# A hybrid encoder block on one core: the opening's transfers as contiguous blocks, and three pieces of the second feed-forward in another form

## The chip, the cores and the metric

The kernel runs on one core of a Trainium2 chip. Its time is the device time of one execution in microseconds. An execution that the hardware profiler recorded gives the rows quoted here; line numbers such as L157 are lines of the kernel before.

## The reference

One layer on a residual stream x of 256 tokens by 2048 features, all in float32:

```
x = x + 0.5 * swiglu(rms_norm(x, ffn1_norm), ffn1_w_up, ffn1_w_down)     # D_FF = 5632
h = rms_norm(x, mix_norm); proj = h @ w_in                               # two recurrent branches, gated
x = x + merged @ w_out
x = x + cross_attention(rms_norm(x, xattn_norm), rms_norm(mem, mem_norm), wq, wkv, wo)
x = x + 0.5 * swiglu(rms_norm(x, ffn2_norm), ffn2_w_up, ffn2_w_down)
return rms_norm(x, final_norm)

def swiglu(h, w_up, w_down):
    gate, up = split(h @ w_up, 2);  return (silu(gate) * up) @ w_down
```

The change lies in the start of the first feed-forward and in the weights of the second.

## The kernel before

**Precision.** A float32 operand is split into a high part (ACT, L156: a copy into the matmul's number type) and a low part (VectorE, L157: the original less the high part). A product takes three matmuls: high by high, low by high (both at L593, or L587 in the opening) and high by low (L595, or L590).

**The feed-forward.** The up-projection runs in 11 groups of 512 hidden columns. A group has 8 pieces; a piece is a block of weights of 128 partitions by 2048 columns (1 MB), in four quarters of 512 columns, and belongs to two of x's 16 feature tiles. The order of pieces, and of the down-projection's pieces put between the groups, is written out in `ffn_order`: in the second feed-forward a group runs its pieces as 1, 3, 4, 0, 2, 5, 6, 7; behind groups 1 and 2 stand two down pieces each, behind later groups four.

A "fast" piece does a two-by-two block product with seven products in place of eight. For this it needs differences of the weight quarters. Where they come from depends on the piece:

- made on the spot: the 1024 KB piece is loaded (L308) and VectorE computes the four differences, in three operations, at L314 (1024 columns), L316 and L317 (512 each), into a second tile;
- "ready": the differences were computed during the middle of the kernel (`make_ahead`, L210: a load on POOL's queue, four subtractions at L218, a store to DRAM at L219). The feed-forward then loads three quarters of the piece (768 KB, L304) and the prepared tile (1024 KB, L306), and VectorE only splits (1536 columns at L157, then twice 1024).

`sums_ready` (L88) says which pieces of the second feed-forward are ready: in groups 0 to 2 all fast ones, in odd later groups all but 0, 5, 7, in even ones all but 0, 3, 5, 7. That makes 58 tiles prepared ahead. In `beside` they are taken up in turns, every two to four weight pieces of the middle stage.

**Tiles and queues.** All weight loads go out on SP's queue, two pieces ahead of the product (`weights`). The loaded tiles come from two pools, three and (in the second feed-forward) two tiles, taken in a fixed turn; a piece of either form takes two. A load waits until the last reader of the tile's earlier content is done. The high parts have three tiles of 2048 columns, and a fast piece uses two of them. The engines run their own queues in order. The order in each queue is made by the compiler's scheduler, but SP, ACT and VectorE keep the written order for the first eight weight pieces (`manual_schedule`).

**The opening.** `xT` holds x by features: per partition 512 columns (x's first block: feature tiles 0 and 1, 256 tokens each), 16 columns of gains, then the other blocks. `head_x(0)` loads the first 528 columns in one transfer (L735), and ACT makes the high parts of both halves, z = 0 and 1, scaled by the gain (L738). `prepare` then takes the first weight piece in four quarters (L290): the high part of quarter 0 is made by VectorE (L292), which also makes the low part of x's two halves (L295) and of the quarter (L297); the other quarters go through `split`. The following three weight pieces are also loaded in quarters, each after another block of x (L742, 512 columns); for x's later use ACT scales the blocks at L534 and splits them at L156.

The first piece's products pair x's first half with quarters 0 and 1 and its second half with quarters 2 and 3 (`PRODUCTS["plain"]`).

Of the kernel before, what the change touches and what calls it, by code (L numbers as in the profile page):

```python
# [8 lines left out]
F32 = mybir.dt.float32  # L9
F32R = mybir.dt.float32r  # L10
ACT = mybir.ActivationFunctionType
ALU = mybir.AluOpType

P = 128
T = 256
D = 2048
KT = D // P
# [69 lines left out]

def sums_ready(name, e):  # L88

    made = () if e[1] < 3 else (0, 5, 7) if e[1] % 2 else (0, 3, 5, 7)  # L90
    return name == "ffn2" and e[0] == "fast" and e[2] not in made


# [1 line left out]
def block_kernel(ctx: ExitStack, tc: tile.TileContext, xT, xin, memT, vec, gfin, bgate, lruw, wu1, wd1, win, wv,  # L95
                 wg, wab, wout, wq, wk, wvm, wo, wu2, wd2, out_):
    nc = tc.nc
    pe, dve, act, sp = nc.tensor, nc.vector, nc.scalar, nc.sync
# [56 lines left out]
    def split(h, l, raw):  # L155
        done["high"] = act.activation(h, raw, ACT.Copy).ins  # L156
        done["low"] = dve.tensor_tensor(out=l, in0=raw, in1=h.bitcast(F32), op=ALU.subtract).ins  # L157
# [120 lines left out]
    def prepare(src, kind, cuts=1):  # L278

        if kind == "added":  # L280
            raw, l = begun.pop(0)
            h = hp.tile([P, 2048], F32R, name="h", tag="h")
            done["high"] = act.activation(h, raw, ACT.Copy).ins
            return h, l
        raw = raw_tile()
        n = 2048 // cuts
        if kind == "plain":
            h, l = split_tiles()
            for a in range(0, 2048, n):
                sp.dma_start(raw[:, a:a + n], src[:, a:a + n])  # L290
                if opening and not pairs1[0][1] and not a and cuts > 1 and len(pairs1) == 1:
                    dve.tensor_scalar(out=h[:, :n], in0=raw[:, :n], scalar1=1.0, scalar2=None, op0=ALU.mult)  # L292
                    for z in range(2):
                        v = [t[:, z * T:(z + 1) * T] for t in opening]
                        dve.scalar_tensor_tensor(out=v[2], in0=v[0], scalar=gain1(z), in1=v[1].bitcast(F32),  # L295
                                                 op0=ALU.mult, op1=ALU.subtract)
                    done["low"] = dve.tensor_tensor(out=l[:, :n], in0=raw[:, :n], in1=h[:, :n].bitcast(F32),  # L297
                                                    op=ALU.subtract).ins
                else:
                    split(h[:, a:a + n], l[:, a:a + n], raw[:, a:a + n])  # L300
            return h, l
        if kind == "ready":
            src, t = src
            sp.dma_start(raw[:, 512:], src[:, 512:])  # L304
            td = raw_tile()
            sp.dma_start(td, t)  # L306
        else:
            sp.dma_start(raw, src)  # L308
            if "raw2" in scoped:
                td = raw_tile()  # L310
            else:
                td = scoped["wide"].tile([P, 2048], F32, name="td", tag="wide")
            two = [v[:, a:a + 1024].rearrange("p (i n) -> p i n", i=2) for v, a in ((td, 0), (raw, 512))]
            dve.tensor_tensor(out=two[0], in0=raw[:, None, :512].broadcast_to([P, 2, 512]), in1=two[1],  # L314
                              op=ALU.subtract)
            dve.tensor_tensor(out=td[:, 1024:1536], in0=raw[:, 1024:1536], in1=td[:, :512], op=ALU.subtract)  # L316
            dve.tensor_tensor(out=td[:, 1536:], in0=raw[:, 1536:], in1=td[:, 1024:1536], op=ALU.subtract)  # L317
        h, l = split_tiles()
        if kind != "fast added":
            split(h[:, 512:], l[:, 512:], raw[:, 512:])  # L320
        else:
            act.activation(l[:, 512:], raw[:, 512:], ACT.Copy, scale=-1.0)
            nc.gpsimd.dma_start(l[:, 512:], src[:, 512:], accum_op=ALU.add)
            done["high"] = act.activation(h[:, 512:], raw[:, 512:], ACT.Copy).ins
        th = hp.tile([P, 2048], F32R, name="h", tag="h")
        if "wide" in scoped:
            tl = scoped["wide"].tile([P, 2048], F32R, name="tl", tag="wide")
        else:
            tl = lp.tile([P, 2048], F32R, name="tl", tag="l")
# [389 lines left out]
    pairs1, sq1 = [], TokenSquares()  # L719

    xq, sums1, opening = {}, [], []

    def gain1(k):
        return opening[0][:, 512 + k:513 + k]

    def head_x(p):

        q = p // 2
        if p % 2 == 0:
            xq[q] = slot(name="xf"), slot(name="xg"), []  # L730
        src, xg, out = xq[q]
        a = p % 2 * 512
        if p == 0:
            opening.append(slot(name="xf")[:, :528])
            sp.dma_start(opening[0], xT[:, :528])  # L735
            opening.extend((slot(F32R, "xh"), slot(F32R, "xl")))
            for z in range(2):
                act.activation(opening[1][:, z * T:][:, :T], opening[0][:, z * T:][:, :T], ACT.Copy, scale=gain1(z))  # L738
            sums = None
            pairs1.append(((opening[1], opening[2]), None))  # L740
            return
        sp.dma_start(src[:, a:a + 512], xT[:, 16 + p * 512:16 + (p + 1) * 512])  # L742
        if p == 1:
            operand_pairs([opening[0][:, :512]], gain1, 0, xg, out, made=opening[1:])
            pairs1[0] = out[-1]
        if p == 6:
            sp.dma_start(vt[:, :small_n], vec[:, :small_n])
        sums = operand_pairs([src[:, a:a + 512]], gain1, q, xg, out)
        if p % 2:
            sums1.append(sums)  # L750
        pairs1.append(out[-1])
# [111 lines left out]
    v = [scoped["extra"].tile([P, 1024], F32, name=f"v{t}", tag="extra") for t in range(2)]  # L863
# [468 lines left out]
def _layout(inputs):  # L1332
    import numpy as np

    a = {k: np.asarray(v) for k, v in inputs.items()}
# [26 lines left out]
    def first(gain, t):  # L1362

        t = features(t)
        return np.concatenate([t[:, :512], vector(gain), t[:, 512:]], axis=1)

    def vector(t):
        return t.reshape(-1, P).T
# [7 lines left out]
    for name in ("ffn1_norm", "mix_norm", "xattn_norm", "mem_norm", "ffn2_norm", "hgrn_norm", "conv_w", "conv_b"):  # L1376
# [7 lines left out]
    s, t = np.arange(P)[:, None] % 32, np.arange(32)[None, :]  # L1384
# [13 lines left out]
        "gfin": np.ascontiguousarray(np.broadcast_to(a["final_norm"], (P, D))),  # L1398
        "bgate": bgate,
        "lruw": np.ascontiguousarray(lruw).reshape(P, 16 * P),  # L1400
        "wu1": up(a["ffn1_w_up"][0]), "wd1": down(a["ffn1_w_down"][0]),
        "win": win, "wv": rows(w[:, 2048:3072]), "wg": wg, "wab": wab, "wout": rows(a["w_out"][0]),
        "wq": columns(a["xattn_wq"][0]), "wk": columns(wkv[:, :D]), "wvm": rows(wkv[:, D:]),
        "wo": rows(a["xattn_wo"][0]),
# [23 lines left out]
```

## Time and profile before

| what | value |
|---|---|
| median of 3 runs | 2415.89 us (2414.18 to 2417.0) |
| the profiled execution | 2416.49 us |
| its span, first to last instruction | 2414.7 us |
| instructions | 30834 |
| mean granted TensorE clock | 0.999 |
| moved by DMA | 684.34 MB, mean 283 GB/s |

The page lists for each engine its busy time and the number of instructions; PEld is TensorE's loading of weights, which overlaps its matmuls; DVE is VectorE. In rows of the timeline the first number is the start from the beginning of the span, the second how long it took, both in us; in brackets at the end stands the idle time of the engine just before, and what ended it. A row can hold several instructions (x4). In the rows by line stand busy us and mean ns of one, then the idle time before them and its releasers.

### The profile page before, as it was taken

How to read it: one execution, taken by the hardware profiler on the slowest of the kernel's cores; microseconds unless marked ns; L12 is line 12 of the kernel's file. 1: busy time of each engine (PE TensorE's matmuls, PEld its weight loads, DVE VectorE, ACT ScalarE, POOL GpSimd, SP SyncE). 2: the span in 40 equal slices, each digit the busy share in tenths (PEclk: the TensorE clock that was granted, in tenths of full speed). 3: DMA queues.
4: the chain of work that ended last, by engine and by line, in shares of the span. 5: the costliest groups of instructions: out<-in, count | busy, mean ns of one | idle time of the engine just before them, and what ended most of it. 6: DMA issues, size and time to landing. Idle time of an engine off the chain costs nothing.

```text
span 2414.7 us, 30834 instructions
## 1 busy us (share of the span) xinstructions
PE 2400.2 (99%) x12102; PEld 2003.2 (83%) x12102; DVE 2051.1 (85%) x2293; ACT 1466.9 (61%) x1502; POOL 102.3 (4%) x166
## 2 busy tenths in 40 slices
PE   9999999999999999999999999999999999999998
PEld 8888888888888888888888888888888788788887
DVE  7999999999866878688876777777789899999995
ACT  8567777777654454476434555455676666666664
POOL 0000000000000000000000000000000000000000
PEclk9999999999999999999999999999999999999999
DMA  8578999899858776878998899876797878787873
GB/s 314 195 230 257 276 277 277 275 274 271 270 215 320 275 284 245 302 283 317 349 332 332 305 356 343 320 291 242 262 348 303 285 283 288 257 293 277 290 276 146
DMA packets 102386, 684.34 MB, mean 283 GB/s; under 512 B 11360, under 2 KB 11616, under 8 KB 29280
## 3 DMA queue, kind: packets, MB, share of 16 engines
q1 hardware_dynamic: 78912, 519.82, 57.5%
q0 software_dynamic: 23328, 162.54, 22.2%
q8 instruction: 95, 1.56, 0.2%
q14 instruction: 51, 0.42, 0.0%
HBM read 619.40 MB, written 62.91 MB: 283 GB/s over the span
## 4 chain that ended last, share of the span: by engine, by line
PE 98%; DMA 1%; ACT 1%; DVE 0%; issue 0%; SPq 0%; ACTq 0%; DVEq 0%
PE acc L593 36%; PE acc L595 18%; PE acc L342 11%; PE acc L367 8%; PE acc L368 8%; PE acc L370 8%; PE acc L345 6%; PE acc L633 1%; PE acc L510 1%; DMA raw<-wu 1%; ACT h L156 0%; PE acc L949 0%; PE acc L1248 0%; PE acc L1202 0%; DMA raw<-t 0%; PE acc L1064 0%
## 5 line engine op out<-in xcount | busy, mean ns | idle before, releaser
L156 ACT ACTIVATE h<-raw 128x2048 fp32r<-128x2048 f32 (+3 forms) x577 | 866.8, 1528 | 622.4 <-PE acc L368 215.2
L157 DVE TENSOR_TENSOR l<-raw,h 128x2048 fp32r<-128x2048 f32 (+2 forms) x405 | 833.2, 2059 | 208.8 <-ACT h L156 208.1
L593 PE MATMUL acc<-h,xh 128*128 128x512 f32 x1220 | 475.0, 391 | 2.1 <-ACT h L156 2.1
L593 PE MATMUL acc<-h,xl 128*128 128x512 f32 x1220 | 473.0, 390 | 0.0
L593 PE MATMUL acc<-h,hidop 128*128 128x512 f32 x1408 | 352.1, 391 | 2.3 <-ACT h L156 2.3
L367 PE MATMUL acc<-h,ops 128*128 128x512 f32 x832 | 326.4, 392 | 0.0
L368 PE MATMUL acc<-h,ops 128*128 128x512 f32 x832 | 324.4, 390 | 0.0
L593 PEld LDWEIGHTS acc<-h,hidop 128*128 128x128 f32 x1408 | 262.4, 188 | 56.8 <-ACT h L156 3.2
L342 PE MATMUL acc<-ops,h 128*128 128x512 f32 x1152 | 277.5, 392 | 0.0
L593 PEld LDWEIGHTS acc<-h,xh 128*128 128x128 f32 x1220 | 229.0, 188 | 54.8 <-ACT h L156 7.0
L593 PEld LDWEIGHTS acc<-h,xl 128*128 128x128 f32 x1220 | 229.1, 188 | 46.6
L342 PEld LDWEIGHTS acc<-ops,h 128*128 128x128 f32 x1152 | 211.4, 188 | 41.3
L157 DVE TENSOR_TENSOR tl<-raw,h 128x1024 fp32r<-128x1024 f32 x172 | 203.6, 1218 | 14.5 <-ACT h L156 14.2
L370 PE MATMUL acc<-l,ops 128*128 128x512 f32 x832 | 205.6, 389 | 0.0
L156 ACT ACTIVATE h<-td 128x1024 fp32r<-128x1024 f32 x140 | 146.7, 1055 | 82.2 <-DVE td L314 31.1
L595 PE MATMUL acc<-l,hidop 128*128 128x512 f32 x704 | 190.4, 389 | 0.0
L370 PEld LDWEIGHTS acc<-l,ops 128*128 128x128 f32 x832 | 156.2, 188 | 32.4
L367 PEld LDWEIGHTS acc<-h,ops 128*128 128x128 f32 x832 | 156.2, 188 | 32.2
L368 PEld LDWEIGHTS acc<-h,ops 128*128 128x128 f32 x832 | 156.3, 188 | 31.4
L595 PE MATMUL acc<-tl,xh 128*128 128x512 f32 x624 | 178.1, 391 | 0.1
L157 DVE TENSOR_TENSOR tl<-td,h 128x1024 fp32r<-128x1024 f32 x140 | 170.0, 1219 | 8.4 <-ACT h L156 7.5
L595 PE MATMUL acc<-l,xh 128*128 128x512 f32 x600 | 165.6, 390 | 0.0
(262 smaller groups left out, 2493.0 us busy)
## 6 DMA issues: line engine op xcount, KB each, us to landing
raw<-wu SPq DMA_DIRECT2D x114, 1024.0 KB, 6.4
raw<-wd SPq DMA_DIRECT2D x88, 1024.0 KB, 6.4
prep<-wu POOLq DMA_DIRECT2D x58, 1024.0 KB, 6.6
t<-prep POOLq DMA_DIRECT2D x58, 1024.0 KB, 5.7
raw<-t SPq DMA_DIRECT2D x58, 1024.0 KB, 6.9
raw<-wu SPq DMA_DIRECT2D x58, 768.0 KB, 5.2
raw<-win SPq DMA_DIRECT2D x40, 1024.0 KB, 5.0
raw<-wg SPq DMA_DIRECT2D x32, 1024.0 KB, 5.0
```

The source lines that it names most:

```text
L156: done["high"] = act.activation(h, raw, ACT.Copy).ins
L157: done["low"] = dve.tensor_tensor(out=l, in0=raw, in1=h.bitcast(F32), op=ALU.subtract).ins
L342: pe.matmul(acc, h[:, k * P:(k + 1) * P], xs[k], start=k == 0, stop=False)
L345: done["product"] = pe.matmul(acc[:, :T], l[:, k * P:(k + 1) * P], xs[k][:, :T], start=False, stop=k == KT - 1).ins
L367: pe.matmul(accs[t], x[:, t * P:][:, :P], h[j], start=first and j == 0, stop=False)
L368: pe.matmul(accs[t], x[:, T + t * P:][:, :P], h[j], start=False, stop=False)
L370: done["product"] = pe.matmul(accs[t], x[:, t * P:][:, :P], l[j], start=False, stop=last and j == 3).ins
L510: pe.transpose(acc[:, z * T + t * P:][:, :P], tile[:, t * 512 + (2 * y + z) * P:][:, :P], ident)
L593: pe.matmul(acc, a, b, start=start, stop=False)
L595: pe.matmul(acc, ah, bl, start=False, stop=stop)
L633: pe.transpose(acc[:, z * T + t * P:][:, :P], hid[t][:, (2 * y + z) * P:][:, :P], ident)
```

## The change

**The layouts.** The host writes `xT` as one flat array of contiguous blocks: the 16 gain columns with x's first half (272 columns), x's second half (256), then seven blocks of 512. The first four pieces of the first up-projection's weights are written quarter by quarter, so that a quarter of 128 by 512 is one contiguous 256 KB block; before, its rows of 2 KB lay 8 KB apart.

**The opening's order.** SP issues x's first half, quarters 0 and 1, x's second half, then quarters 2 and 3. On ACT, the high part of x's second half is made behind quarter 1's; on VectorE its low part likewise.

**The second feed-forward.** In groups 1 and 2, piece 6 is made on the spot, not ready. In group 3, piece 0 is ready, not made on the spot. Groups 0 and 4 to 10 are as they were. 57 tiles are prepared ahead.

```diff
 def sums_ready(name, e):
-    made = () if e[1] < 3 else (0, 5, 7) if e[1] % 2 else (0, 3, 5, 7)
+    made = {0: (), 1: (6,), 2: (6,), 3: (5, 7)}.get(e[1], (0, 5, 7) if e[1] % 2 else (0, 3, 5, 7))
     return name == "ffn2" and e[0] == "fast" and e[2] not in made
...
             for a in range(0, 2048, n):
-                sp.dma_start(raw[:, a:a + n], src[:, a:a + n])
-                if opening and not pairs1[0][1] and not a and cuts > 1 and len(pairs1) == 1:
+                first = opening and len(pairs1) == 1 and cuts > 1
+                quarter = src.rearrange("p (a n) -> (p a) n", n=n)[a // n * P:][:P] if cuts > 1 else src
+                sp.dma_start(raw[:, a:a + n], quarter)
+                if first and not a:
                     dve.tensor_scalar(out=h[:, :n], in0=raw[:, :n], scalar1=1.0, scalar2=None, op0=ALU.mult)
-                    for z in range(2):
-                        v = [t[:, z * T:(z + 1) * T] for t in opening]
-                        dve.scalar_tensor_tensor(out=v[2], in0=v[0], scalar=gain1(z), in1=v[1].bitcast(F32),
-                                                 op0=ALU.mult, op1=ALU.subtract)
+                    remainder(0)
                     done["low"] = dve.tensor_tensor(out=l[:, :n], in0=raw[:, :n], in1=h[:, :n].bitcast(F32),
                                                     op=ALU.subtract).ins
                 else:
                     split(h[:, a:a + n], l[:, a:a + n], raw[:, a:a + n])
+                if first and a == n:
+                    sp.dma_start(opening[0][:, 272:], block(272, 256))
+                    rounded(1)
+                    remainder(1)
...
     def gain1(k):
-        return opening[0][:, 512 + k:513 + k]
+        return opening[0][:, k:k + 1]
+
+    def block(a, n):
+        return xT[a * P:(a + n) * P].rearrange("(p n) -> p n", p=P)
+
+    def rounded(z):
+        act.activation(opening[1][:, z * T:][:, :T], opening[0][:, 16 + z * T:][:, :T], ACT.Copy, scale=gain1(z))
+
+    def remainder(z):
+        dve.scalar_tensor_tensor(out=opening[2][:, z * T:][:, :T], in0=opening[0][:, 16 + z * T:][:, :T],
+                                 scalar=gain1(z), in1=opening[1][:, z * T:][:, :T].bitcast(F32), op0=ALU.mult,
+                                 op1=ALU.subtract)
...
-            sp.dma_start(opening[0], xT[:, :528])
+            sp.dma_start(opening[0][:, :272], block(0, 272))
             opening.extend((slot(F32R, "xh"), slot(F32R, "xl")))
-            for z in range(2):
-                act.activation(opening[1][:, z * T:][:, :T], opening[0][:, z * T:][:, :T], ACT.Copy, scale=gain1(z))
+            rounded(0)
...
-        sp.dma_start(src[:, a:a + 512], xT[:, 16 + p * 512:16 + (p + 1) * 512])
+        sp.dma_start(src[:, a:a + 512], block(16 + p * 512, 512))
...
+    def in_quarters(t):
+
+        t[0, :4] = t[0, :4].reshape(4, P, 4, 512).transpose(0, 2, 1, 3).reshape(4, P, 2048)
+        return t
...
-        "wu1": up(a["ffn1_w_up"][0]), "wd1": down(a["ffn1_w_down"][0]),
+        "wu1": in_quarters(up(a["ffn1_w_up"][0])), "wd1": down(a["ffn1_w_down"][0]),
```

More of the change, by code (lines that the diff above doesn't have):

```diff
@@ L741, in head_x @@
             return
-        sp.dma_start(src[:, a:a + 512], xT[:, 16 + p * 512:16 + (p + 1) * 512])
+        sp.dma_start(src[:, a:a + 512], block(16 + p * 512, 512))
         if p == 1:
-            operand_pairs([opening[0][:, :512]], gain1, 0, xg, out, made=opening[1:])
+            operand_pairs([opening[0][:, 16:]], gain1, 0, xg, out, made=opening[1:])
             pairs1[0] = out[-1]
@@ L1364, in first @@
         t = features(t)
-        return np.concatenate([t[:, :512], vector(gain), t[:, 512:]], axis=1)
+        blocks = [np.concatenate([vector(gain), t[:, :T]], axis=1), t[:, T:512]]
+        blocks += [t[:, i:i + 512] for i in range(512, KT * T, 512)]
+        return np.concatenate([b.reshape(-1) for b in blocks])
+    def in_quarters(t):
+        t[0, :4] = t[0, :4].reshape(4, P, 4, 512).transpose(0, 2, 1, 3).reshape(4, P, 2048)
+        return t
     def vector(t):
```

## The prediction

> **What bounds the kernel now.** I read the page first (busy times), then the chain of work that ended last, then the waits of TensorE (us in total, times, longest).
>
> ```profile
> PE 2400.2 (99%) x12102; PEld 2003.2 (83%) x12102; DVE 2051.1 (85%) x2293; ACT 1466.9 (61%) x1502; POOL 102.3 (4%) x166
> PE 98%; DMA 1%; ACT 1%; DVE 0%; issue 0%; SPq 0%; ACTq 0%; DVEq 0%
> PE acc L593 <- ACT h L156: 4.4, 4, 1.6
> PE acc L587 <- ACT h L156: 0.9, 1, 0.9
> ```
>
> TensorE is busy for 99% of the span and is 98% of the chain. The change takes no matmul away, so all that it can win is TensorE's pauses, and they are few: 0.9 us at L587, in the first piece, and 4.4 us in four waits at L593. The question is therefore where each pause comes from, and whether new ones come up. The timeline of TensorE gives their places.
>
> ```profile
> 5.44 0.70 PE L587 MATMUL acc<-h,xh 128*128 128x512 f32 x2 [0.22 <-DVE h L292]
> 7.51 0.73 PE L587 MATMUL acc<-h,xh 128*128 128x512 f32 x2 [0.93 <-ACT h L156]
> ...
> 1887.46 0.61 PE L595 MATMUL acc<-tl,xh 128*128 128x512 f32 x2
> 1889.69 0.50 PE L593 MATMUL acc<-h,xh 128*128 128x512 f32 x1 [1.61 <-ACT h L156]
> 1902.64 0.50 PE L593 MATMUL acc<-h,xh 128*128 128x512 f32 x1 [0.44 <-ACT h L156]
> 1911.55 1.43 PE L593 MATMUL acc<-h,hidop 128*128 128x512 f32 x5 [1.17 <-ACT h L156]
> ...
> 2095.55 0.96 PE L593 MATMUL acc<-h,hidop 128*128 128x512 f32 x3 [1.14 <-ACT h L156]
> ```
>
> The first two rows are the opening. The next four lie in group 3 of the second feed-forward (its pieces run from about 1867 us). The last is alone in a later group, which the change does not touch. A matmul's row is longer than its place in the row of matmuls: the chain has 20 of them in 4.53 us.
>
> ```profile
> 1863.98 4.53 PE acc L593 x20
> ```
>
> That is 0.227 us each, while single rows say 0.39, so each pause is really about 0.16 us longer than its idle column: after the two matmuls from 1887.46 the next was due at 1887.91 and came at 1889.69, which is 1.78. The three pauses of group 3 are 1.61 + 0.44 + 1.17 + 3 x 0.16 = 3.7 us; the opening's is 1.09, besides the late start at 5.44.
>
> **Opening: what is removed, added and moved.** Now one transfer brings 528 columns of x with the gains (264 KB), then four quarters of the first weight piece follow. The change sends 272 columns (136 KB), quarters 0 and 1, then x's other 256 columns (128 KB), then quarters 2 and 3. One issue by SP is added. L738 and L295 work in halves as now, but the second halves stand behind quarter 1's split. L295's second half (0.44 us) is hidden: the matmuls that need it come after twelve others.
>
> ```profile
> 0.74 0.38 SPq L735 DMA_DIRECT2D xf<-xT  x1
> 4.22 0.91 ACT L738 ACTIVATE xh<-xf 128x256 fp32r<-128x256 f32 x2 [1.78 <-DMA xf<-xT]
> 4.86 0.43 DVE L292 TENSOR_SCALAR h<-raw 128x512 fp32r<-128x512 f32 x1 [3.86 <-DMA raw<-wu]
> 6.83 2.01 ACT L156 ACTIVATE h<-raw 128x512 fp32r<-128x512 f32 x3 [1.71 <-DMA raw<-wu]
> 8.74 1.70 ACT L534 ACTIVATE xg<-xf 128x256 f32<-128x256 f32 x4
> 11.01 2.18 ACT L156 ACTIVATE h<-raw 128x512 fp32r<-128x512 f32 x4
> 11.96 0.19 PEld L593 LDWEIGHTS acc<-h,xh 128*128 128x128 f32 x1
> ```
>
> Three landings can be read here: x at 4.22, quarter 0 at 4.86, quarter 1 at 6.83. Quarter 0 came 0.64 us after x, quarter 1 took 1.97 for the same 256 KB. With 128 KB less in front, half of 0.64 is saved: quarter 0 lands at 4.54, and the first matmul starts 0.32 earlier, at 5.12. Quarter 1 then lands at 5.18 if it follows by 0.64, at 6.51 if it still takes 1.97. Its split on ACT takes 2.01 / 3 = 0.67, so TensorE goes on somewhere between 5.85 (no pause left: its four first matmuls last until 6.03) and 7.18. The first piece alone gains at least 0.32 and at most 0.32 + 1.09 = 1.41.
>
> What is late next is ACT: from 6.83 on its rows follow each other without idle to 11.01, the second piece's first split, and TensorE takes that piece up at 11.96. Half of L738 (0.46) now stands in this row of work. So the gain that goes on into the second piece is the advance of quarter 1 less 0.46: 6.83 - 5.18 - 0.46 = 1.2 at best, 0.32 - 0.46 = -0.14 at worst. SP's extra issue (0.38) is hidden by the transfers in flight; if it were not, quarters 2 and 3 would be that much later, still behind ACT. The rate over the first 16 us (40 slices of 0.4 us) says which end is nearer.
>
> ```profile
> GB/s 0 0 0 0 79 121 353 346 339 334 302 138 195 302 271 277 220 261 302 307 215 246 307 358 405 405 405 405 405 410 405 399 410 369 405 389 384 379 379 389
> ```
>
> Nothing moves before 1.6 us, then 340, then a trough of 138 to 307 from 4.4 to 8.8, then 405 with quarters of the same shape. The trough is where quarter 1 waits. Contiguous blocks may or may not fill it; less in front of quarter 1 helps either way. I take 1.1 us, near the upper end since 0.64 is the time that a quarter took outside the trough, and keep -0.1 to 1.4.
>
> The Trainium skill, DMA: Bandwidth & Descriptors, in Latency and other measured facts, has copies slowed by a large row pitch in HBM and advises contiguous tiles. Its slow pitches start at 512 KiB; here rows are 8 KB apart, and the 405 GB/s slices run at that pitch, so the rule does not reach this case; by it all 1.2 us would come. The skill's Perfetto Trace Analysis, DMA Optimizations, speaks against the split: DMAs under 2 KB carry an overhead each, and x's rows go from 2112 B to 1088 and 1024. If half a block took as long as the whole, the sum below would be smaller by 0.3.
>
> That the gain lasts needs cover too: VectorE is busy for 88.89 of the 89 us that follow.
>
> ```profile
> 39.00:128.00 89.00, 89.00 (x401) 73.35 (x400) 88.89 (x109) 56.73 (x54) 0.00 (x0) 1.00 0.55 203
> ```
>
> TensorE never pauses there, but a TensorE that is early could meet a VectorE that is not. VectorE's work starts with the same transfers, so I leave the 1.1 whole and count its loss in the range.
>
> **Second feed-forward.** A piece in the "ready" form loads 768 KB and 1024 KB of prepared differences; in the "fast" form it loads 1024 KB, and VectorE makes the differences at L314, L316, L317. Group 3's piece 0 goes from fast to ready; piece 6 of groups 1 and 2 goes from ready to fast. The price of one piece:
>
> ```profile
> 1882.51 1.22 DVE L314 TENSOR_TENSOR raw<-raw 128x1024 f32<-128x1024 f32 x1
> 1883.64 1.75 DVE L157 TENSOR_TENSOR l<-raw,h 128x1536 fp32r<-128x1536 f32 x1
> 1885.31 0.68 DVE L316 TENSOR_TENSOR raw<-raw,raw 128x512 f32<-128x512 f32 x1
> 1885.91 1.22 DVE L157 TENSOR_TENSOR tl<-raw,h 128x1024 fp32r<-128x1024 f32 x1
> 1887.05 0.69 DVE L317 TENSOR_TENSOR raw<-raw,raw 128x512 f32<-128x512 f32 x1
> 1889.67 1.76 DVE L157 TENSOR_TENSOR l<-raw,h 128x1536 fp32r<-128x1536 f32 x1 [1.94 <-ACT h L156]
> ```
>
> Three operations, 1.22 + 0.68 + 0.69 = 2.6 us of VectorE, against 768 KB of transfers. Which of the two is short, the busy times by stretch show (after TensorE and its loads: VectorE, ACT, POOL, clock, DMA share, GB/s):
>
> ```profile
> 1789.00:1809.00 20.00, 20.00 (x90) 16.57 (x89) 15.72 (x12) 13.01 (x12) 0.00 (x0) 1.00 1.01 411
> 1838.00:1858.00 20.00, 20.00 (x90) 16.57 (x89) 16.32 (x12) 13.08 (x13) 0.00 (x0) 1.00 1.01 423
> 1867.00:1887.00 20.00, 20.00 (x93) 16.55 (x92) 19.35 (x18) 10.39 (x10) 0.00 (x0) 1.00 0.70 247
> 1887.00:1912.00 25.00, 21.64 (x91) 16.39 (x90) 21.73 (x21) 16.45 (x15) 0.00 (x0) 1.00 0.75 282
> ```
>
> The ends of groups 1 and 2 (first two rows) have full queues and 4.3 and 3.7 us of free VectorE; group 3 (last two) has a full VectorE and queues at 0.7. The edit moves work from the full side to the free one in all three. In groups 1 and 2 I count the 2.6 us at nothing: the free VectorE time hides it; without that cover it would be 2.6 each.
>
> Group 3's pauses hang on the VectorE queue. The chain:
>
> ```profile
> 1877.51 1.76 DVE l L157
> 1879.70 8.35 DMA raw<-wu
> ...
> 1891.35 1.23 DVE tl L157
> 1892.59 6.94 DMA raw<-t
> 1899.64 2.96 ACT h L156 x3
> ```
>
> A VectorE split frees a tile, only then is the load issued, and it lands after TensorE wanted it; the next load hangs on the next split. Without piece 0's three operations VectorE is 2.6 us earlier from 1882.5 on. The ready form needs two loads for piece 0, whose second tile is free when the previous pieces are split, which by the order of the five tiles is about 1874 (an estimate), in queues at a 0.70 share; 768 KB at 247 GB/s cost 3.2 us of them, at 411 1.9. Piece 2's load then shares with less that is late, and VectorE's wait of 1.94 goes too or is halved. With 2.6 to 4.5 us of advance in VectorE's queue, the pauses at 1902 and 1911 (0.6 and 1.3) are covered; the first (1.78) has the load of piece 2 as its cause, which the same tile release starts. I take 3.5 of the 3.7; bounds 0 (only the place of the pause changes) and 3.7.
>
> Fifty-seven tiles are prepared ahead in place of 58, with the turns shifted by one; the stages where that is done have no pause in the waits above, so nothing.
>
> **Sum.** 1.1 + 3.5 + 0 = 4.6 us. The profiled execution took 2416.49 (span 2414.7, 1.8 around it), so 2411.9; the median shown is 0.6 lower, and from it I forecast **2411.3 us**, 0.19% less. A measurement of this kernel can tell about 0.2% from no change, 4.8 us: the forecast stands just at that line.
>
> **Rivals.** *More than the sum*: the pause at 2095.55 (1.14 + 0.16) goes as well, because what is early in group 3 stays early, and the opening gives its 1.4: 1.4 + 3.7 + 1.3 = 6.4, 2409.5. Against it: ACT's wait there is in a group with unchanged work.
>
> *Only one edit pays*: quarter 1 stays in its trough or VectorE eats the advance by 128 us, or piece 2's load stays late. Group 3 alone gives 2412.4, the opening alone 2414.8. For it: piece 2's two transfers hang on one tile release, which lies before 1882.5 and is not moved.
>
> *Slower*: an L314 stands at the head of VectorE's queue and waits for its 1024 KB, in groups 1 and 2, where the queues are at 1.01.
>
> ```profile
> L314 DVE TENSOR_TENSOR raw<-raw 128x1024 f32<-128x1024 f32 x28 | 34.1, 1219 | 7.2 <-DMA raw<-wu 7.2
> ```
>
> Now 28 such operations wait 7.2 us in all. Behind it stand the splits of piece 7 and of the down pieces, which free tiles, so SP's loads wait too. It decides once that wait and the 2.6 exceed the 4.3 or 3.7 us of free time. Then each group would pause as group 3 did: 2 x 3.7 - 1.1 = 6.3 more, 2422.2 (with group 3 no better). Against it: later groups run three or four fast pieces each with one pause in seven groups.
>
> *It does not do what it says*: the order in each queue is the scheduler's, and if it puts piece 0's loads late, group 3 is as before: the second rival's time.
>
> **Chances.** The forecast with its own range 2409.9 to 2412.9: 0.55, of it 0.32 past the 0.2% line (2411.06). More than the sum: 0.14. One edit or less: 0.13. Slower: 0.18, of it 0.01 within 0.2%. Faster by over 0.2%: 0.32 + 0.14 = 0.46; within: 0.23 + 0.13 + 0.01 = 0.37; slower: 0.17. The range 2408.0 to 2418.0 leaves out the slower case and some 0.02 below.
>
> **What would show it.** Quarter 1's split on ACT before 6 us and no idle at L587; VectorE without the L314 row in group 3's piece 0 and no TensorE idle from 1867 to 1912; in groups 1 and 2, L314 rows without idle ahead and VectorE near 18.5 of 20. I am wrong if TensorE shows a new wait for ACT or VectorE between 1789 and 1867, or near 128 us.

## The result and the profile after

| what | before | after |
|---|---|---|
| median | 2416.49 us (2414.18 to 2418.37) | 2411.79 us (2410.6 to 2414.4) |
| ratio of after to before | | 0.9982, 95% interval 0.9976 to 0.9988 |
| the profiled execution, its span | 2416.49, 2414.7 | 2412.53, 2410.8 |
| instructions, moved by DMA | 30834, 684.34 MB | 30823, 681.45 MB |

The kernel is 0.18% faster, some 4.3 us, and the forecast was 2411.3. The total came out; its terms did not all. In the kernel after, the lines that matter have moved: L587 is L590, L590 is L593, L593 is L596, L595 is L598, L290 is L292, L292 is L294, L304/L306/L308 are L307/L309/L311, L314/L316/L317 are L317/L319/L320, L680 is L683, L738 is L733, L534 is L537. Kernels made from the old one keep the old numbers.

From the page of after, the busy times:

```profile
PE 2399.4 (100%) x12102; PEld 2004.9 (83%) x12102; DVE 2048.3 (85%) x2292; ACT 1466.6 (61%) x1502; POOL 101.3 (4%) x164
```

TensorE is busy 0.8 us less than before in a span that is 3.9 us shorter: what went is mostly idle time. The waits of TensorE in after, and the places of its pauses in its timeline:

```profile
PE acc L596 <- ACT h L156: 2.6, 4, 1.2
```

```profile
4.92 0.92 PE L590 MATMUL acc<-h,xh 128*128 128x512 f32 x2
...
11.12 0.51 PE L596 MATMUL acc<-h,xh 128*128 128x512 f32 x1 [0.29 <-ACT h L156]
...
1801.66 0.50 PE L596 MATMUL acc<-h,xh 128*128 128x512 f32 x1 [0.90 <-ACT h L156]
...
1853.47 0.50 PE L596 MATMUL acc<-h,xh 128*128 128x512 f32 x1 [1.18 <-ACT h L156]
...
2091.90 0.96 PE L596 MATMUL acc<-h,hidop 128*128 128x512 f32 x3 [0.19 <-ACT h L156]
```

The wait at the first piece (0.9 us) is gone. Of the waits at the later pieces, the three of group 3 are gone; two new ones stand in groups 1 and 2, and the one at 2095 has shrunk from 1.14 to 0.19. Taking matmuls of equal number in both traces, after is ahead by 1.06 us at the second piece, by 0.70 to 0.77 from 48 to 1400 us, by 0.83 at 1752. Then it loses 1.2 in group 1 and 1.7 in group 2, gains 4.7 in group 3, 0.95 at 2095 and 0.33 later: 3.9 us in all, the difference of the spans.

The stretches of the three groups in after (1768.7 to 1818, to 1867, to 1912; in order: length, TensorE, its loads, VectorE, ACT, POOL, clock, DMA share, GB/s):

```profile
1768.70:1818.00 49.30, 48.40 (x218) 39.69 (x217) 45.81 (x43) 34.95 (x33) 0.00 (x0) 1.00 0.85 311
1818.00:1867.00 49.00, 47.82 (x214) 39.03 (x213) 45.83 (x42) 32.73 (x30) 0.00 (x0) 1.00 0.83 305
1867.00:1912.00 45.00, 45.00 (x204) 37.24 (x204) 43.40 (x41) 31.90 (x29) 0.00 (x0) 1.00 0.80 294
```

VectorE still has more than 3 us free in groups 1 and 2, though TensorE pauses there. VectorE's own rows show that it did not wait for data at the new operations; here the first of them in group 1 of after:

```profile
1793.99 1.22 DVE L317 TENSOR_TENSOR raw<-raw 128x1024 f32<-128x1024 f32 x1
...
1800.69 1.76 DVE L157 TENSOR_TENSOR l<-raw,h 128x1536 fp32r<-128x1536 f32 x1 [1.48 <-ACT h L156]
```

L317 (the old L314) has no idle time ahead of it. Over the whole span the made-on-the-spot form waits less than before, with one more of them:

```profile
L317 DVE TENSOR_TENSOR raw<-raw 128x1024 f32<-128x1024 f32 x29 | 35.4, 1219 | 5.4 <-DMA raw<-wu 5.4
```

What idles VectorE (1.48 us) is ACT, and ACT waits for a load. The chain of work through that place in after, and SP's queue:

```profile
1788.87 1.70 DVE l L157
...
1790.59 0.33 SPq L309
...
1790.96 8.11 DMA raw<-wu
...
1799.17 0.49 ACT h L156
```

```profile
1790.96 0.43 SPq L307 DMA_DIRECT2D raw<-wu  x1
```

This is piece 7, a ready piece behind piece 6, which is now fast. Its prepared tile (L309) is issued ahead of its own weights (L307), although the weights are wanted first. L309 waits for the tile that VectorE's split at 1788.87 frees; L307 stands behind it, shares the queues with 1024 KB of it, and takes 8.11 us. TensorE goes on at 1801.66. In group 2 the same pair goes out at 1841.90 and 1842.28, and L307's load takes 8.6 us. The profile puts ACT's wait there (until 1850.99) down to TensorE; by its 8.6 us the load landed at about the same moment. In the kernel before one place has this order: group 3's piece 2, the 8.35 us load of the prediction's chain, ahead of the pause at 1889.69. The new form of piece 6 brings that place into groups 1 and 2; the new form of piece 0 takes it out of group 3.

### The profile page after: what moved, and what is told of

Read it like the earlier page. It is cut to its first block, busy times and chain, and to the rows that moved or that the text cites. A ratio compares the mean times of both kernels' runs of the same rounds, so it can differ in the third digit from the quotient of the medians.

```text
span 2410.8 us, 30823 instructions
## 1 busy us (share of the span) xinstructions
PE 2399.4 (100%) x12102; PEld 2004.9 (83%) x12102; DVE 2048.3 (85%) x2292; ACT 1466.6 (61%) x1502; POOL 101.3 (4%) x164
## 2 busy tenths in 40 slices
DMA packets 102098, 681.45 MB, mean 283 GB/s; under 512 B 11328, under 2 KB 11840, under 8 KB 29248
## 3 DMA queue, kind: packets, MB, share of 16 engines
q8 instruction: 95, 1.56, 0.2%
## 4 chain that ended last, share of the span: by engine, by line
PE 97%; DVE 1%; DMA 1%; ACT 1%; issue 0%; SPq 0%; ACTq 0%
PE acc L596 36%; PE acc L598 18%; PE acc L345 11%; PE acc L370 8%; PE acc L371 8%; PE acc L373 8%; PE acc L348 6%; PE acc L636 1%; PE acc L513 1%; DMA raw<-wu 1%; DVE tl L157 0%; DVE l L157 0%; PE acc L962 0%; ACT h L156 0%; PE acc L1261 0%
## 5 line engine op out<-in xcount | busy, mean ns | idle before, releaser
L596 PE MATMUL acc<-h,xh 128*128 128x512 f32 x1220 | 476.0, 392 | 2.4 <-ACT h L156 2.4
L596 PE MATMUL acc<-h,xl 128*128 128x512 f32 x1220 | 473.6, 390 | 0.0
L596 PE MATMUL acc<-h,hidop 128*128 128x512 f32 x1408 | 352.3, 391 | 0.2 <-ACT h L156 0.2
L596 PEld LDWEIGHTS acc<-h,hidop 128*128 128x128 f32 x1408 | 262.8, 188 | 54.1 <-ACT h L156 0.6
L596 PEld LDWEIGHTS acc<-h,xh 128*128 128x128 f32 x1220 | 229.1, 188 | 55.5 <-ACT h L156 7.7
L596 PEld LDWEIGHTS acc<-h,xl 128*128 128x128 f32 x1220 | 229.3, 188 | 46.3 <-DVE xl L157 0.2
L598 PE MATMUL acc<-l,hidop 128*128 128x512 f32 x704 | 190.9, 390 | 0.0
L598 PE MATMUL acc<-tl,xh 128*128 128x512 f32 x624 | 177.6, 392 | 0.0
L598 PE MATMUL acc<-l,xh 128*128 128x512 f32 x600 | 165.7, 390 | 0.0
```

What stands on the lines that cost most here:

```text
L596: pe.matmul(acc, a, b, start=start, stop=False)
L598: pe.matmul(acc, ah, bl, start=False, stop=stop)
```

## The experiments

Two theories at the start. **T**: the order of the two loads of a ready piece makes a pause; the change moved the place. **V**: VectorE's row of work, with the tiles it frees, sets how much is lost; the order only says where. A third came after the first four runs. **D**: what group 3 needs is less to transfer in groups 1 and 2. Each kernel was timed beside the kernel before on the same chip. Intervals of 11 executions reach 0.09% (2.2 us) to either side, so the medians tell 3 us apart and not 1; the traces must do the rest, and each of them is one execution.

### The opening alone

```diff
-    made = {0: (), 1: (6,), 2: (6,), 3: (5, 7)}.get(e[1], (0, 5, 7) if e[1] % 2 else (0, 3, 5, 7))
+    made = () if e[1] < 3 else (0, 5, 7) if e[1] % 2 else (0, 3, 5, 7)
```

> The changed kernel with the old rule for the prepared pieces: the opening's edits alone. Theory A (the two edits add up): TensorE's second piece starts about 1 us earlier and 0.7 us of it is left at 48 us, as in the trace of the changed kernel; the pauses of group 3 (1.6 + 0.4 + 1.2 us idle) stand as before. Time 0.7 us under the kernel before, about 2415.8. Theory B (the opening's advance helps group 3 too): over 2 us under it.

2415.74 us against 2415.79: ratio 0.9998 (0.9990 to 1.0007). Nothing that the measurement can see. ACT's timeline in this kernel says why:

```profile
4.68 0.63 ACT L156 ACTIVATE h<-raw 128x512 fp32r<-128x512 f32 x1 [1.24 <-DMA raw<-wu]
...
8.11 1.28 ACT L156 ACTIVATE h<-raw 128x512 fp32r<-128x512 f32 x2 [2.00 <-DMA raw<-wu]
9.29 1.69 ACT L537 ACTIVATE xg<-xf 128x256 f32<-128x256 f32 x4
```

Quarter 1 is split at 4.68, earlier than my best bound. But ACT waits 2.00 us for quarter 2 and splits it only at 8.11, and its row of work, L537 onwards, begins at 9.29, later than the old kernel's 8.74. All transfers together are not slow here: they move 334 GB/s from 4.4 to 8.8 us, against 249 in before. Another transfer is the late one now, and no run tells why. TensorE starts the second piece at 12.22, against 12.18 in before.

### The second feed-forward alone

The new rule of `sums_ready` in the kernel before (the diff above, reversed).

> The kernel before with the new rule for the prepared pieces alone. Theory A (the edits add up): no pause in group 3, a pause of about 1 us in group 1 and one in group 2, about 3.2 us under the kernel before, 2413.3; the opening as before. Theory B: the pauses of groups 1 and 2 come of TensorE's advance from the opening; then they are missing here and it is 5 us under.

2413.16 us: 0.9989 (0.9980 to 0.9997), 2.6 us less. So the rule of the feed-forward gains by itself. In this trace the pauses stand where after has them, in groups 1 and 2, with none in group 3 (0.57 idle at 1802.18, 1.64 at 1854.28). The execution traced here took 2416.08, 2.9 us over this kernel's median; the places of the pauses are read from it, and not the gain.

It reached the second piece at 11.13, as early as after's 11.12, with the old opening; quarter 1 was split at 5.61, not 6.83. The same opening can be 1 us apart from one trace to another.

### The order of the two loads, in the kernel before

```diff
-            sp.dma_start(raw[:, 512:], src[:, 512:])
+            own = sp.dma_start(raw[:, 512:], src[:, 512:]).ins
             td = raw_tile()
-            sp.dma_start(td, t)
+            with tc.issue_after(own): sp.dma_start(td, t)
```

It swaps two rows of SP's queue, the pair of group 3's piece 2.

> The kernel before, with one thing changed: the load of a piece's own weights stands ahead of the load of its prepared tile on SP's queue, always. In the kernel before they stand the other way round at one place, piece 2 of group 3, behind piece 0. Theory T (order of issue): the pause of 1.78 us at that piece goes, since its 768 KB load no longer waits behind the other's tile; the later ones of group 3 shrink with it; 2 to 4 us under the kernel before. Theory V (VectorE's three operations): the pauses stay within 0.5 us in sum, the time is that of the kernel before.

2415.46 us: 0.9998 (0.9989 to 1.0007). The pause at 1889 is gone; the load that it waited for now takes 4.2 us, not 8.3. But the time has come back 16 to 20 us later in group 3. The chain behind the largest pause (1.49 idle):

```profile
1899.43 1.23 DVE tl L157
...
1900.67 7.01 DMA raw<-wd
...
1907.77 1.92 ACT h L156
...
1909.73 4.52 PE acc L593 x12
```

From 1880 to 1900 this chain runs through VectorE almost without a break; a VectorE split frees the tile for the down piece's load, which is late. The order of issue set the place of the pause, as T says, but not the loss, as V says. (Part of this execution's loss is a slower clock, told below.)

### The same order, in the kernel after

The same edit; it swaps the pairs of groups 1 and 2.

> The changed kernel, with the own weights' load always ahead of the prepared tile's. In the changed kernel they stand the other way round at two places, piece 7 of groups 1 and 2, behind piece 6. Theory T (order of issue): the pauses of 1.06 and 1.34 us there go, 2 to 2.4 us under the changed kernel, about 2409.5. Theory V (VectorE's 2.6 us in groups 1 and 2 are not hidden): the pauses stay, 2411.8.

2414.43 us: 0.9994 (0.9985 to 1.0003); no better than after. The pauses of groups 1 and 2 are gone (the two loads take 6.6 and 5.4 us), so the order was their immediate cause, but the 2.4 us did not come. The traced execution took 2412.65, 1.8 us under the median, and no less than after's. A new pause stands at the end of group 3 (1908.34, 1.56 idle), and its chain shows something new:

```profile
1905.89 0.60 ACT hid L683
1906.49 1.81 ACT h L156
...
1908.34 1.66 PE acc L596 x6
```

ACT's queue holds the copy of one of the group's finished sums out of its accumulator (L683) ahead of the split that TensorE needs next. L683 can only run when TensorE ends that sum; the split then takes 1.81 us, and TensorE stands still for most of it.

### The kernel after once more

No edit.

> The changed kernel once more, beside the variants below on one chip. Its pauses from 1768 to 1930 us should come out again as one of about 1 us each in groups 1 and 2 and none in group 3, and the time 3 to 5 us under the kernel before. If the opening's advance is steady, the second piece's first matmul stands at 11.1 us again; if it hangs on when the slow stretch of the transfers falls, anywhere from 11.1 to 12.2.

2412.63 us: 0.9986 (0.9977 to 0.9995). In this execution group 1 pauses for 1.86 us and group 2 not at all. Which of the two pauses is a matter of the execution; that they do is not. The order of the two loads is the same each time; what differs is how long the load behind takes. Here it is, in us from issue to landing, beside TensorE's pause behind it. The last four rows are runs told below; the run with two pieces in group 2 is left out, since its group 2 differs.

| trace | group 1: load, pause (idle) | group 2: load, pause (idle) |
|---|---|---|
| after | 8.1, 0.90 | 8.6, 1.18 |
| after once more | 9.1, 1.86 | 6.7, none |
| the feed-forward alone | 7.8, 0.57 | 9.1, 1.64 |
| only groups 1 and 2 | 8.0, 0.78 | 6.5, none |
| one piece in group 3 | 7.6, 0.39 | 7.8, 0.41 |
| order alone | 8.2, 0.98 | 6.4, none |
| contiguous blocks alone | 8.2, 0.98 | 6.3, none |

The pause grows with the load, and up to 6.7 us there is none. Why the same two transfers take longer one time than another, no run tells.

### Only group 3, and only groups 1 and 2

```diff
-    made = {0: (), 1: (6,), 2: (6,), 3: (5, 7)}.get(
+    made = {0: (), 1: (), 2: (), 3: (5, 7)}.get(
```

> The changed kernel, but piece 6 of groups 1 and 2 stays ready: of the rule's edits only that of group 3 is left, and 59 tiles are prepared. Theory V (VectorE's time sets it: 2.6 us less in group 3, nothing added elsewhere): no pause in groups 1 to 3, 2 to 2.4 us under the changed kernel. Theory D (the relief of the transfers in groups 1 and 2 is needed for group 3): pauses of 1 us or more stay in group 3, and the time is that of the changed kernel or worse.

2413.33 us: 0.9990 (0.9982 to 0.9999), 2.6 us less than before. Groups 1 and 2 do not pause; group 3 does, at 1899.65 (0.55) and 1909.46 (1.58). V's empty group 3 did not come, and D expected such pauses. The first hangs, as the one at 1902 in before, on a load that starts behind a VectorE split, though the three operations of piece 0 are gone from VectorE's queue:

```profile
1889.28 7.26 DMA raw<-t
...
1899.65 1.88 PE acc L596 x7
```

The second pause is again L683 ahead of the split. ACT's timeline here, and then in after:

```profile
1907.01 0.60 ACT L683 ACTIVATE hid<-acc 128x512 f32<-128x512 f32 x1 [2.71 <-PE acc L598]
1907.50 4.66 ACT L156 ACTIVATE h<-raw 128x2048 fp32r<-128x2048 f32 x3
```

```profile
1905.96 2.86 ACT L156 ACTIVATE h<-raw 128x2048 fp32r<-128x2048 f32 x2 [1.81 <-DMA raw<-wd]
1908.73 0.57 ACT L683 ACTIVATE hid<-acc 128x512 f32<-128x512 f32 x1
```

In after two splits stand ahead of L683. The order came out otherwise from another list of pieces, and the pause goes with the order.

```diff
-    made = {0: (), 1: (6,), 2: (6,), 3: (5, 7)}.get(
+    made = {0: (), 1: (6,), 2: (6,), 3: (0, 5, 7)}.get(
```

> The changed kernel, but group 3's piece 0 is made on the spot as before: of the rule's edits only those of groups 1 and 2. Theory V: the pauses of groups 1 and 2 (2.4 us) come on top of group 3's 3.7 or more, 2 us or more over the kernel before. Theory D: group 3's pauses shrink to 2 us or less, and it is no slower than before.

2414.89 us: 0.9996 (0.9988 to 1.0005). Group 1 pauses (0.78), and group 3 loses 1.7 (4.05 in before, 2.89 with the opening alone), the largest part at 1909.60 behind L683. V has the pauses of groups 1 and 2 come on top of group 3's, and they do not: this kernel has the edits of groups 1 and 2 without the relief of group 3, and is no slower than before. D fits better. The order of loads at group 3's piece 2 is before's here (1878.53 and 1878.91), and its load takes 7.4 us, but TensorE does not pause: the order makes a load late, and does not by itself make a pause.

### One piece fewer in group 3, one more in group 2

```diff
-    made = {0: (), 1: (6,), 2: (6,), 3: (5, 7)}.get(
+    made = {0: (), 1: (6,), 2: (6,), 3: (7,)}.get(
```

> The changed kernel with group 3's piece 5 ready too, so that only piece 7 is made on the spot there (58 tiles). Theory V: group 3 has no pause in the changed kernel, so nothing is won there; the pauses of groups 1 and 2 stay; the changed kernel's time within 1 us. If something of group 3 is still short, over 1 us under it.

2412.34 us: 0.9985 (0.9977 to 0.9994), equal to after within the intervals. Its pauses in groups 1 to 3 are small (0.39 and 0.41 idle, none in group 3; a split again stands ahead of L683), and its profiled span is the shortest, 2409.8.

```diff
-    made = {0: (), 1: (6,), 2: (6,), 3: (5, 7)}.get(
+    made = {0: (), 1: (6,), 2: (3, 6), 3: (5, 7)}.get(
```

> The changed kernel with a second piece of group 2 (piece 3) made on the spot, 2.6 us more for VectorE and 768 KB less to load. Theory V (VectorE has no free time left there): TensorE pauses 2 us or more longer in groups 2 and 3, about 2.6 us over the changed kernel. Theory D (the transfers are short): no longer pauses, the changed kernel's time or less.

2416.80 us: 1.0000 (0.9991 to 1.0009); the gain is used up. The pauses came late: 1911.63 (1.58, L683 ahead of the split at 1909.18) and in a later group, where the other traces pause for 0.39 us at most:

```profile
2034.49 0.96 PE L596 MATMUL acc<-h,hidop 128*128 128x512 f32 x3 [1.04 <-ACT h L156]
```

V is nearer in the time than D: it put this kernel 2.6 us over the changed one, and two kernels with after's pieces took 2412.90 and 2411.83 on this chip. But V's places are not right, since group 2 does not pause at all. That group 2 has room for one such piece and not for two, and that what it owes is paid groups later, is a reading and not shown; the traced execution (2417.57) also pauses for 0.87 us at 258.84, in the first feed-forward, which the edit does not touch.

### One piece in group 3, with the own weights first

The edits of two kernels above together (`3: (7,)`, and the order of the two loads).

> The changed kernel with piece 5 of group 3 ready too (as in the run before with one piece made on the spot in group 3) and the own weights' load always ahead of the prepared tile's. Theory T for the place and V for the sum: the pauses of 0.55 and 0.57 us in groups 1 and 2 go, and VectorE has room in group 3, so that no pause comes up there: about 1 us under the run without the load order, 3.5 to 5.5 under the kernel before. If the pause at the end of group 3 (1.7 us, when the load order was changed alone) comes up here too, VectorE's room is not what decides it.

2414.64 us: 0.9994 (0.9985 to 1.0003). The pauses of groups 1 to 3 are at most 0.31 idle each, as T has it. The 3.5 to 5.5 us under the kernel before did not come: a load of down-projection weights is late behind group 3:

```profile
1915.41 2.30 DVE l L157
...
1917.86 12.22 DMA l<-wd
...
1930.12 1.20 PE acc L598 x4
```

For the third time the "right" order of issue removed the pauses that it aimed at, or nearly, and gained nothing that the times show.

### The opening's order and its layouts apart

```diff
-                quarter = src.rearrange("p (a n) -> (p a) n", n=n)[a // n * P:][:P] if cuts > 1 else src
+                quarter = src[:, a:a + n]
...
-        return xT[a * P:(a + n) * P].rearrange("(p n) -> p n", p=P)
+        return xT[:, a:a + n]
```

(with `xT` and the weights written as before: new order, strided rows)

> The changed kernel with the old, strided layouts of x and of the first weight pieces; the opening's order of transfers as changed. Theory O (fewer bytes in front do it): the first half of x is used by ACT at about 2.9 us and quarter 0 by VectorE at about 4.0, as in the changed kernel. Theory C (contiguous blocks do it): with 128 KB less in front only 0.3 us is won, ACT starts at 3.9 and VectorE at 4.5. Either way quarters 2 and 3 are split at 7 to 8 us, and the time is that of the changed kernel within 1 us.

2412.90 us: 0.9986 (0.9977 to 0.9995).

```diff
-            sp.dma_start(opening[0][:, :272], block(0, 272))
+            sp.dma_start(opening[0], block(0, 528))
...
-                if first and a == n:
-                    sp.dma_start(opening[0][:, 272:], block(272, 256))
-                    rounded(1)
-                    remainder(1)
```

(contiguous blocks, x's first block whole and both halves made at once, as before)

> The changed kernel with contiguous blocks, but x's first block whole (528 columns, one block) and the old order of transfers. Theory O: ACT starts at 4.0 to 4.4 us and VectorE at 4.7 to 5.1, as in the kernel before. Theory C: about 3.2 and 3.9. Either way the time is that of the changed kernel within 1 us.

2411.83 us: 0.9983 (0.9974 to 0.9992). Both times hold the feed-forward's gain too, and they are equal within the intervals. The landings show which part does what. Order alone, ACT and VectorE:

```profile
2.99 0.51 ACT L733 ACTIVATE xh<-xf 128x256 fp32r<-128x256 f32 x1 [0.56 <-DMA xf<-xT]
6.21 0.63 ACT L156 ACTIVATE h<-raw 128x512 fp32r<-128x512 f32 x1 [2.71 <-DMA raw<-wu]
```

```profile
4.62 0.43 DVE L294 TENSOR_SCALAR h<-raw 128x512 fp32r<-128x512 f32 x1 [3.62 <-DMA raw<-wu]
```

Contiguous blocks alone (the first row makes both halves; L534 here is after's L537):

```profile
3.59 0.91 ACT L730 ACTIVATE xh<-xf 128x256 fp32r<-128x256 f32 x2 [1.16 <-DMA xf<-xT]
5.44 2.01 ACT L156 ACTIVATE h<-raw 128x512 fp32r<-128x512 f32 x3 [0.95 <-DMA raw<-wu]
7.36 1.69 ACT L534 ACTIVATE xg<-xf 128x256 f32<-128x256 f32 x4
```

```profile
4.24 0.43 DVE L294 TENSOR_SCALAR h<-raw 128x512 fp32r<-128x512 f32 x1 [3.24 <-DMA raw<-wu]
```

x's half block comes at 2.9 to 3.0 in either layout: that is the smaller transfer's doing, as theory O has it. Contiguity, theory C, brings whole x from 4.22 to 3.59 and quarter 0 behind it from 4.86 to 4.24; in the new order it brings quarter 0 from 4.62 to between 3.87 and 4.30, and quarter 1 from 6.21 to between 4.68 and 5.00. So each part does something, and neither theory alone is right. In the one execution of contiguous blocks with whole x, ACT's row starts earliest of all (7.36), TensorE starts the second piece at 10.79, and its 1000th matmul at 224.88; the earliest of the other kernels is 225.57. One execution, and a time equal to after's: a hint, not a result.

## Why the prediction was right, and where it was not

The time was right; the terms were not, and part of the agreement is luck. Two terms were too favourable: the opening, and groups 1 and 2. In the two traces of before and after they were made up for by group 3, which gave 4.7 us in place of 3.5, and by 1.3 us behind it, in groups that the forecast left as they were. The prediction's own sign of being wrong also came: new waits for ACT at 1801.66 and 1853.47, between 1789 and 1867. VectorE reached 16.55 and 16.86 us of 20 there, not 18.5.

Of the two edits, the feed-forward's rule alone shows a gain (0.9989); the opening alone shows none (0.9998). So the rival "only one edit pays" (2412.4 with group 3 alone) is not excluded: after's interval, taken of 2416.49, is 2410.7 to 2413.6 and holds both.

**Opening, 1.1 us: mis-sized.** The landings are better than its bounds: quarter 1 was split at 4.74 (5.18 to 6.51 foreseen), the first matmul came at 4.92 (5.12), and the pause at the first piece went. Nor did x's half block take as long as the whole, the price that the prediction held open: 2.1 us from issue to landing, against 3.5. Earlier than 4.91 the first matmul does not come in any trace, though quarter 0 reaches VectorE anywhere from 3.87 to 4.30 in the new opening. TensorE is busy until then with 18 matmuls on a tile of ones (L143), which the prediction left out:

```profile
1.05 4.21 PE L143 MATMUL warm<-ones 128*128 128x128 f32 x18 [1.05 <-DVE ones L140]
```

After's rows on ACT:

```profile
4.74 0.63 ACT L156 ACTIVATE h<-raw 128x512 fp32r<-128x512 f32 x1 [1.32 <-DMA raw<-wu]
6.34 0.51 ACT L733 ACTIVATE xh<-xf 128x256 fp32r<-128x256 f32 x1 [0.97 <-DMA xf<-xT]
...
8.18 1.69 ACT L537 ACTIVATE xg<-xf 128x256 f32<-128x256 f32 x4
```

What failed is the step "the gain that goes on into the second piece is the advance of quarter 1 less 0.46". It took ACT's row to run without idle behind quarter 1. It does not: ACT now waits for x's second half (0.97) and then for quarter 2 (0.17, at 7.03), and begins L537 0.56 us earlier than before, though quarter 1 was split 2.09 earlier. And 1.1 was worked out against one execution. The old opening reached the second piece at 12.18, 11.13 and 11.93 in the three traces that have it (mean 11.75); the new one in nine traces at 11.12 to 12.22 (mean 11.48). At the 1000th matmul the means are 225.97 and 225.90. The differences of these means, 0.27 and 0.07 us, are less than the scatter of single traces, about 1 us. So no gain of the opening is resolved; what there is lies inside the bounds of -0.1 to 1.4, near the end that I did not choose. Some of the earlier first matmul is given back at once, since the first matmuls may run at half rate (below).

**Group 3, 3.5 of 3.7 us: right in size, the cause right in part.** All three pauses went. The first hung on the order of two loads, which the prediction did not see; the run with own weights first shows it. The second hung, by its chain, on a load behind VectorE's split, as I said. But VectorE's three operations are not the whole cause: without them a pause by the same chain stays (only group 3, 1899.65), and with them group 3 loses 1.7 us when only groups 1 and 2 are edited, in place of the 2.89 with the opening alone. The third I put down to VectorE's queue too; in before it hung on ACT's order. The chain of before:

```profile
1908.84 0.24 PE acc L595
...
1909.10 0.60 ACT hid L680
1909.70 1.81 ACT h L156
...
1911.55 0.50 PE acc L593
```

The six profiles in which a split stands ahead of that copy (after twice, the feed-forward alone, one piece in group 3, order alone, contiguous blocks alone) have no pause there. In the eight others the copy comes first, and all pause there, by 0.23 to 1.58 us idle; in one of them, the kernel before with own weights first, the load for the split came later still. No run changed this order alone, so that it is the whole price of that pause is read from chains, not shown by an edit.

**Groups 1 and 2, nothing: wrong as put.** "The free VectorE time hides it" looked at VectorE's busy time alone. VectorE made the differences without waiting, as foreseen, but the load behind the fast piece was late: 1.06 + 1.34 us of pauses (start to start), 2.9 with small losses around them. The rival "slower" had the groups right and the mechanism wrong: no operation of that line waited for its data there. In the time of the whole kernel no cost of the edit is seen: without it (only group 3) the kernel took 2413.33, with it 2412.63, on the same chip, and the difference is not resolved. What after loses in groups 1 and 2 it does not lose at group 3's end.

**The pause at 2095, unchanged in the forecast.** It went from 1.30 to 0.35, which was a part of the rival "more than the sum". Over the six traces with after's rule of pieces it is 0.35, 0.39, 0.45, 0.47, 1.00 and 1.29; with the old rule 0.60, 0.99 and 1.30. It shrinks more often than not, and varies by as much.

**Prepared tiles, nothing: right.** VectorE makes them between 711 and 1700 us; after's lead is 0.70 us ahead of that stretch and 0.83 behind it, so it changes by 0.13 us.

**The sum over groups.** Add TensorE's pauses of over 0.2 us, start to start, from 1768 to 1932. Old rule: 4.05 in before, 2.89 with the new opening. After's rule: 2.40, 2.53, 2.02, 1.14, 1.14. One piece in group 3: 1.12. Only group 3: 2.45. Only groups 1 and 2: 2.61. Two pieces in group 2: 2.90. Own weights first: 1.73 in after, 2.88 with one piece in group 3. What sets this sum is not settled, and it does not follow the times closely: after's rule has from 1.14 to 2.53. The order of issue alone does not set it: three tries moved pauses and gained nothing. VectorE's work alone does not: the kernel before and the one with one piece in group 3 both make three pieces on the spot in these groups (three in group 3; one in each), with 0.15% (3.6 us) between their times. The likeliest reading, argued and not shown, is that tiles and splits are late by a little all along, and that each order of the queues decides at which next narrow place TensorE pays for it.

## What to carry to other kernels

An engine's free time in a stretch does not hide work if that work changes which load is issued when, and which instruction stands ahead in another engine's queue: look for the loads that share a tile's release, and for copies out of the accumulators queued ahead of the next split. When a pause is taken out of a row of work that is nearly full, look for it further on before you count the gain. Profile the unchanged program more than once before you take a difference of 1 us from two traces; here the start of one and the same opening varied by that much.

## What the runs showed of the hardware

The transfers of the first 9 us have a slow stretch, and contiguous blocks fill a part of it. From 4.4 to 8.8 us the rate is 249, 267 and 274 GB/s in the three traces of the old opening and 271 in order alone, all with strided rows; it is 289 to 341 in the ten traces with contiguous blocks. Rates in before and then in contiguous blocks alone, the highest:

```profile
4.40:8.80 4.40, 3.25 (x15) 2.31 (x14) 3.10 (x6) 2.58 (x6) 0.00 (x0) 1.00 0.95 249
```

```profile
4.40:8.80 4.40, 4.40 (x21) 3.49 (x20) 3.71 (x7) 3.34 (x8) 0.00 (x0) 1.00 1.01 341
```

After's rate there is 289 GB/s, and from 8.8 to 16 us before and after have 389 and 392: there the layout made no difference.

A pause can cost more than its length. In the kernel before with own weights first, behind pauses of 0.36 and 1.49 us, the granted clock fell to half:

```profile
1905.00:1909.70 4.70, 2.69 (x10) 1.53 (x9) 3.06 (x4) 2.73 (x4) 0.00 (x0) 0.99 0.92 347
1909.70:1912.40 2.70, 2.67 (x6) 2.15 (x7) 2.69 (x2) 2.70 (x3) 0.00 (x0) 0.50 0.86 352
```

Six matmuls in 2.7 us, where twelve fit: about 1.3 us beside the pause. Single pauses of 1.56 and 1.86 us in other traces left the clock at 1.00. That two close together did it here is a reading of this one place. The Trainium skill, TensorE: Matmul & The Clock Gate, in Part 1 on the clock gate, describes a gate that judges TensorE by how busy it was in free-running windows of about 3.4 us, and lets half the pulses through after an idle one. The trace agrees in the half rate and in its length (1909.7 to about 1913.0); but TensorE was not idle for a whole window here.

In the opening, TensorE's first matmuls at 4.92 also ran at half rate in some executions. With the opening alone:

```profile
4.92 1.20 PE L590 MATMUL acc<-h,xh 128*128 128x512 f32 x2
5.91 1.05 PE L590 MATMUL acc<-h,xl 128*128 128x512 f32 x2
```

The two from 5.91 to 6.77 start 0.43 us apart, against 0.227 later, while the clock's column says 1.00 for that stretch; the two records differ, and no run here tells why.
